# A two-block transformer kernel on one core: the first stage laid out by features

## Chip, cores and metric

The kernel runs on one core of one Trainium2 chip. Its time is the device time of one execution in microseconds (us); the median of several executions is given. Engines are named as in the profile: PE is the matrix engine, DVE the vector engine, ACT the scalar engine, POOL is GpSimd, and SP issues the transfers.

## What is computed

Two transformer blocks on a sequence of 512 tokens with 1024 features, all in float32. Only the head of the first block is touched by the change:

```python
cs = silu(c)                                      # c: (1, 1024)
shift, scale, gate = split(cs @ w_mod + b_mod, 3) # w_mod: (1024, 3072)
h = x * (1 + scale) + shift                       # x: (512, 1024)
q, k, v, r, a_lr = split(h @ gla_w_in, ...)       # gla_w_in: (1024, 3088)
# gated linear attention with 4 heads (keys of 128, values of 256 features),
# layer norm, a gated convolutional MLP with its own modulation;
# second block: a retention layer and an attention layer on latent keys
```

## The kernel before

**Products.** A float32 operand is kept as two parts, `hi` and `lo` (`split`: a cast on ACT, then a subtraction on DVE). A product of two such operands is three matmuls into the same PSUM accumulator, `hi*hi`, `hi*lo` and `lo*hi` (`mm3`, lines 137 to 139). A weight tile is loaded as `raw`, cast by ACT into `wsp` (L97) and completed by DVE (L98, the `lo` part). The product of 128 features with a tile of 512 columns is thus three matmuls of 512 columns.

**First stage** (`gla_start`). It goes over the features in four quarters of 256. Per quarter, `scales` loads eight 128-row slices of the 256 columns of `scale` and of `shift` (`ms`), multiplies each by its value of silu(c) and adds it to `macc` (L487, eight instructions on DVE). `macc` then holds 128 partial sums per column, one on each partition. Four transposes on PE (L359) and a reduction on DVE (L360) turn them into columns (`mc`) that lie along partitions. The quarter of x (`xq`) arrives with tokens on partitions, and eight transposes on PE (L509) bring its features there; ACT applies scale and shift from PSUM twice (L513, once into `hT` hi and once into `xv`), and DVE forms the `lo` part (L514). Then come the projections of this quarter into six PSUM banks: v of the first two heads (four banks, one for each block of 128 tokens), q and k of head 0 (two banks). The other two banks serve the transposes.

**After it**: `gla_a` (24 matmuls with the 16 gate columns `was`), `gla_r` (96 matmuls with the output gates), the decays (`gla_decay`: four float32 matmuls L576, exponential and logarithm on ACT, then L587), and the heads. `gla_qk` projects q and k of a further head, 48 matmuls for each head. `gla_inner` of a head holds a chain of narrow products and small DVE work (`qd`, `ki`, `kt`, `af`, `at`, `sf`, `st`), `gla_outer` the outputs `po`. The place of the program where the heads begin reads

```python
p0 = prep(0)
raw += self.gla_qk(xT, (1,))
p1 = prep(1)
place(3)
i0 = self.gla_inner(ph, p0, vh(0), tril)
raw += self.gla_qk(xT, (2,))
i1 = self.gla_inner(ph, p1, vh(1), tril)
raw += self.gla_qk(xT, (3,))
```

`place` puts in six further pieces of the modulation (`mod_chunk`: four loads `rawm`, eight DVE instructions on `macc` each). They share the four `raw` buffers with the weights. A scheduler makes each engine's order out of the written program; each engine then executes its own list in order. All loads are issued by SP in one list; a load waits there for its buffer, and no more than eight loads are under way at a time.

Of the kernel before, what the change touches and what calls it, by code (L numbers as in the profile page):

```python
# [10 lines left out]
F32 = mybir.dt.float32  # L11
F32R = mybir.dt.float32r
# [6 lines left out]
P = 128  # L19
T = 512  # L20
# [48 lines left out]

class Pair:  # L70
    """hi and lo parts of an operand whose contraction runs over k-tiles of 128 partitions"""
# [8 lines left out]
class Kern:  # L80
# [5 lines left out]
    # ------------------------------------------------------------------ helpers  # L86
# [36 lines left out]
    def wsubs(self, w, c0, c1, k0=0, k1=None, gain=None, pool=None, main=0):  # L123
        """weights w[k0*128:k1*128, c0:c1] in pieces; the first `main` ones always from the main pool"""
# [16 lines left out]
    def psum(self, nacc):  # L141
        """PSUM banks: nacc for the accumulators of projections, the others for all else"""
# [41 lines left out]
    def proj_f(self, xT, tiles, evict, halves=1, nk=8, width=P):  # L184
        """features on partitions: tiles yields the pieces of one feature tile; evict(n, psum[width, 512 tokens])"""
# [23 lines left out]
    def rsqrt(self, v):  # L209
        """1/sqrt(v) for v[128, n] > 0, in float32"""  # L210
# [15 lines left out]
    def transpose_split(self, dst, src, b, split_copy=True):  # L226
        """src [128 tokens, 1024] -> the columns of block b of the k-tiles in dst (Pair tiles [hi|lo][128, 4, 512])"""
# [20 lines left out]
    # ------------------------------------------------------------------ program  # L248
# [5 lines left out]
    def run(self):  # L254
        tc, nc = self.tc, self.nc
        with ExitStack() as ctx:
# [4 lines left out]
            with self.psum(6) as self.ps:  # L261
                next(gla)
# [16 lines left out]
    def setup(self, ph):  # L279
        nc, a = self.nc, self.a  # L280
        cr = ph.tile([8, P], F32, name="cr")
        nc.sync.dma_start(cr, a["c"].rearrange("o (k p) -> (o k) p", p=P))
# [4 lines left out]
        nc.vector.memset(self.ones, 1.0)  # L287
        self.cs = self.cons.tile([P, 8], F32, name="cs")
        cst = ph.tile([8, P], F32, name="cst")
        nc.scalar.activation(cst, cr, AF.Silu)  # L290
        ps = self.aux()
        nc.tensor.transpose(ps[:, :8], cst, self.ident[:8, :8])
        nc.vector.tensor_copy(self.cs, ps[:, :8])
        self.res = [None] * NB
        self.col = {}

    def vectors(self, ph):
        """vectors over features as columns of 128 partitions"""
# [30 lines left out]
    def mod_chunk(self, i, c0, pool=None, tag="raw", bufs=0):  # L329
        """[128, 512] whose column sums are (silu(c) @ mod_w[0, i] + mod_b[0, i])[c0:c0 + 512]"""  # L330
# [18 lines left out]
    def mod_bcast(self, acc):  # L349
        """column sums on all partitions: PSUM [128, 512]"""  # L350
# [4 lines left out]
    def mod_cols(self, acc, out):  # L355
        """column sums as columns: out[128, 4]"""
# [11 lines left out]
    # ------------------------------------------------------------------ GLA  # L368
    def gla(self):
        nc, a, tc = self.nc, self.a, self.tc  # L370
        w = a["gla_w_in"][0]
        with ExitStack() as ctx:
# [27 lines left out]
            with tc.tile_pool(name="gla_core", bufs=1, reuse_waits="tile") as ph:  # L400
# [22 lines left out]
                raw += self.gla_qk(xT, (1,))  # L423
# [25 lines left out]
            # scale and shift of the sublayer that follows  # L449
# [15 lines left out]
    def gla_start(self, ph, out):  # L465
        """x * (1 + scale) + shift, features on partitions, a quarter of the features at a time, and the first
        projections on each quarter: v of the first pair of heads, q and k of the first head"""
        nc, a = self.nc, self.a
        w = a["gla_w_in"][0]
        tl, xT = self.new_hT()  # L470
        accs = [self.acc() for _ in range(6)]
        Q = 256

        def scales(q):
            """1 + scale and shift of a quarter as columns [128, 4], and the quarter of x"""
            c0 = q * Q
            acc = self.mod.tile([P, 512], F32, tag="macc", name="macc", bufs=self.MACC)
            nc.gpsimd.memset(acc, 0.0)
            for j, c in enumerate((1024 + c0, c0)):
                nc.sync.dma_start(acc[0:1, j * Q:(j + 1) * Q], a["mod_b"][0, 0:1, c:c + Q])  # L480
            for k0 in (0, 4):
                raw = ph.tile([P, 4, 2, Q], F32, tag="ms", name="ms", bufs=5)
                for j, c in enumerate((1024 + c0, c0)):
                    nc.sync.dma_start(raw[:, :, j, :], a["mod_w"][0, 0, k0 * P:(k0 + 4) * P, c:c + Q]
                                      .rearrange("(k p) n -> p k n", p=P))
                for k in range(4):
                    nc.vector.scalar_tensor_tensor(acc, raw[:, k].rearrange("p j n -> p (j n)"),  # L487
                                                   self.cs[:, k0 + k:k0 + k + 1], acc, op0=OP.mult, op1=OP.add)
            xq = self.main.tile([P, NB, Q], F32, tag=f"res{q}", name=f"xq{q}")
            nc.sync.dma_start(xq, a["x"][0][:, c0:c0 + Q].rearrange("(b p) n -> p b n", p=P))  # L490
            mc = self.small(4, "mc")
            self.mod_cols(acc, mc)
            nc.vector.tensor_scalar_add(mc[:, 0:2], mc[:, 0:2], 1.0)
            return mc, xq

        def weights(q):
            c0 = q * Q
            return (self.wload([(0, w[c0:c0 + Q, 1024:1536])], 2, 512),
                    self.wload([(0, w[c0:c0 + Q, 0:P]), (P, w[c0:c0 + Q, 512:512 + P])], 2, 2 * P))

        ahead = [scales(0)]
        ws = [weights(0)]
        for q in range(4):
            mc, xq = ahead.pop(0)
            for i in range(2):
                k = 2 * q + i
                px = self.aux()
                for b in range(NB):
                    nc.tensor.transpose(px[:, b * P:(b + 1) * P], xq[:, b, i * P:(i + 1) * P], self.ident)  # L509
                hi, lo = tl[k // 4][:, 0, k % 4, :], tl[k // 4][:, 1, k % 4, :]  # L510
                v = ph.tile([P, T], F32, tag="t2", name="xv", bufs=2)
                for d in (hi, v):
                    nc.scalar.activation(d, px, AF.Identity, scale=mc[:, i:i + 1], bias=mc[:, 2 + i:3 + i])  # L513
                nc.vector.tensor_sub(lo, v, self.f(hi))  # L514
            if q < 3:
                ahead.append(scales(q + 1))
                ws.append(weights(q + 1))
            wv, wqk = ws.pop(0)
            for b in range(NB):
                for i in range(2):  # L520
                    l = [t[:, b * P:(b + 1) * P] for t in xT.k[2 * q + i]]
# [755 lines left out]
```

## Time and profile before

| what | value |
|---|---|
| median of 3 runs | 1274.15 us (1274.1 to 1274.72) |
| span of the profiled execution, first to last instruction | 1272.2 us |
| PE busy | 1239.5 us, 97% of the span |
| DVE busy | 825.5 us, 65% |
| ACT busy | 526.6 us, 41% |
| data moved | 147.83 MB, mean 116 GB/s |

The profiled execution has no time of its own beside its span, so the sums are made against the span; the median of the runs is 1.95 us above it, which is what lies before the first and after the last instruction, and a saving inside the span is carried over to the median as it is. PE counts as busy from the start of a matmul to its modelled end, and matmuls overlap: one of 512 columns shows 0.39 us, and the next one starts 0.23 us after it.

### The profile page before, as it was taken

Reading aid. Unit: us, or ns where it says so; the run is one execution under the profiler, and the core shown is the slowest. Engines: PE = TensorE matmul, PEld = TensorE weight load, DVE = VectorE, ACT = ScalarE, POOL = GpSimd, SP = SyncE. Lnnn points to the kernel's source line nnn. Section 1 sums busy time; section 2 is a strip of 40 time slices with the busy share of each in tenths; the row PEclk is TensorE's granted clock in tenths of the full one; section 3 lists DMA queues with packets and bytes.
Section 4 is the critical chain, followed back from the end, with each engine's and each line's share of the span. In section 5 each row is a group of like instructions: output and inputs, shape, how many; then the busy total and the mean of one; then the engine's idle time right before and its main releaser. Section 6 shows DMA issues by size and latency. Waiting matters only on the chain.

```text
span 1272.2 us, 16374 instructions
## 1 busy us (share of the span) xinstructions
PE 1239.5 (97%) x6123; PEld 1038.8 (82%) x6123; DVE 825.5 (65%) x1838; ACT 526.6 (41%) x930; POOL 8.8 (1%) x22
## 2 busy tenths in 40 slices
PE   4999999999999999999999999999999999999997
PEld 3778877898888888888788888888888889888886
DVE  6968696788543344454884747647454689686755
ACT  3437344353332123342443343423433447476631
POOL 1000000000000000000000000000000000000000
PEclk9999999999999999999999999999999999999999
DMA  9785262517433333325143232233332333212221
GB/s 313 227 256 173 83 220 67 161 42 226 131 99 99 99 99 100 98 90 162 66 149 91 82 97 80 80 94 92 117 116 99 108 97 96 85 47 73 74 93 67
DMA packets 145695, 147.83 MB, mean 116 GB/s; under 512 B 9223, under 2 KB 106030, under 8 KB 145615
## 3 DMA queue, kind: packets, MB, share of 16 engines
q1 hardware_dynamic: 145614, 146.78, 37.3%
q8 instruction: 48, 0.79, 0.3%
q14 instruction: 33, 0.26, 0.1%
HBM read 140.47 MB, written 6.29 MB: 115 GB/s over the span
## 4 chain that ended last, share of the span: by engine, by line
PE 83%; DVE 5%; ACT 2%; issue 1%; DMA 0%; DVEq 0%; ACTq 0%
PE acc L139 24%; PE acc L137 24%; PE acc L138 24%; PE po L137 1%; PE po L139 1%; PE po L138 1%; PE aux L139 1%; PE aux L137 1%; PE aux L138 1%; DVE wsp L98 1%; PE aux L872 1%; PE aux L1241 1%; PE aux L700 0%; ACT hv L709 0%; DVE rs_t L219 0%
## 5 line engine op out<-in xcount | busy, mean ns | idle before, releaser
L98 DVE TENSOR_TENSOR wsp<-raw,wsp 128x1024 fp32r<-128x1024 f32 (+1 forms) x164 | 196.0, 1196 | 197.1 <-ACT wsp L97 196.8
L97 ACT CAST wsp<-raw 128x1024 fp32r<-128x1024 f32 (+1 forms) x164 | 168.6, 1030 | 314.7 <-PE acc L139 253.6
L137 PE MATMUL acc<-hT,wsp 128*128 128x512 f32 (+1 forms) x640 | 244.6, 382 | 0.0
L139 PE MATMUL acc<-hT,wsp 128*128 128x512 f32 (+1 forms) x640 | 244.0, 381 | 0.0
L138 PE MATMUL acc<-hT,wsp 128*128 128x512 f32 (+1 forms) x640 | 243.5, 380 | 0.0
L137 PE MATMUL acc<-wsp,hT 128*128 128x512 f32 (+2 forms) x448 | 172.8, 386 | 2.6 <-ACT hT L513 2.6
L138 PE MATMUL acc<-wsp,hT 128*128 128x512 f32 (+2 forms) x448 | 171.6, 383 | 0.0
L139 PE MATMUL acc<-wsp,hT 128*128 128x512 f32 (+2 forms) x448 | 169.2, 381 | 0.0
L137 PEld LDWEIGHTS acc<-hT,wsp 128*128 128x128 f32 x640 | 121.0, 189 | 22.7 <-issue 0.8
L138 PEld LDWEIGHTS acc<-hT,wsp 128*128 128x128 f32 x640 | 121.0, 189 | 22.1 <-issue 0.2
L139 PEld LDWEIGHTS acc<-hT,wsp 128*128 128x128 f32 x640 | 120.8, 189 | 22.2
L137 PEld LDWEIGHTS acc<-wsp,hT 128*128 128x128 f32 x448 | 84.7, 189 | 19.0 <-ACT hT L513 3.6
L139 PEld LDWEIGHTS acc<-wsp,hT 128*128 128x128 f32 x448 | 84.1, 188 | 15.2
L138 PEld LDWEIGHTS acc<-wsp,hT 128*128 128x128 f32 x448 | 84.8, 189 | 14.1
L137 PE MATMUL acc<-wsp,uT 128*128 128x512 f32 (+1 forms) x192 | 74.6, 389 | 0.0
L139 PE MATMUL acc<-wsp,uT 128*128 128x512 f32 (+1 forms) x192 | 74.6, 388 | 0.0
L138 PE MATMUL acc<-wsp,uT 128*128 128x512 f32 (+1 forms) x192 | 74.4, 387 | 0.0
L137 PE MATMUL acc<-wsp,p 128*128 128x512 f32 x144 | 56.1, 389 | 0.0
L138 PE MATMUL acc<-wsp,p 128*128 128x512 f32 x144 | 56.1, 389 | 0.0
L139 PE MATMUL acc<-wsp,p 128*128 128x512 f32 x144 | 56.1, 389 | 0.0
L774 DVE SCALAR_TENSOR_TENSOR cv<-acc,cols,cv 128x511 f32<-128x511 f32 x22 | 16.5, 749 | 57.1 <-ACT cv L773 57.1
L342 DVE SCALAR_TENSOR_TENSOR macc<-rawm,cs,macc 128x512 f32<-128x512 f32 x64 | 47.9, 749 | 8.3 <-DMA rawm<-in_mod_w 7.3
(364 smaller groups left out, 2081.4 us busy)
## 6 DMA issues: line engine op xcount, KB each, us to landing
raw<-in_w_in_a SPq DMA_DIRECT2D x48, 512.0 KB
raw<-in_ffn_w_up SPq DMA_DIRECT2D x44, 512.0 KB
rawm<-in_mod_w SPq DMA_DIRECT2D x32, 512.0 KB
raw<-in_gla_w_in SPq DMA_DIRECT2D x22, 512.0 KB
raw<-in_ffn_w_down SPq DMA_DIRECT2D x22, 512.0 KB
ms<-in_mod_w SPq DMA_DIRECT2D x16, 512.0 KB
raw<-in_w_out_a SPq DMA_DIRECT2D x16, 512.0 KB
raw<-in_gla_w_o SPq DMA_DIRECT2D x8, 512.0 KB
```

Source lines behind the costliest of these rows:

```text
L97: nc.scalar.copy(hi, src)
L98: nc.vector.tensor_sub(lo, src, self.f(hi))
L137: mm(out, l[0], r[0], start=first, stop=False)
L138: mm(out, l[0], r[1], start=False, stop=False)
L139: mm(out, l[1], r[0], start=False, stop=last)
L342: nc.vector.scalar_tensor_tensor(acc, raw[:, k, :], self.cs[:, k0 + k:k0 + k + 1], acc, op0=OP.mult, op1=OP.add)
L774: nc.vector.scalar_tensor_tensor(t[:, 1:], p[:, :T - 1], cw[NT + j], t[:, 1:], op0=OP.mult, op1=OP.add)
L872: nc.tensor.transpose(pu[:, b * P:(b + 1) * P], u[:, b, i * P:(i + 1) * P], self.ident)
L1241: nc.tensor.transpose(pt[:, (b - j) * P:(b - j + 1) * P], pr[b][:, j * P:(j + 1) * P], self.ident)
```

## The change

Five arrays are laid out anew outside the kernel, as further inputs: x transposed (`l_x`, features as rows), the scale and shift columns of the first modulation matrix transposed and side by side (`l_mod`, 1024 rows of 2048), their bias as columns (`l_modb`), c as columns (`l_c`), and the weight columns of v of heads 0 and 1, q of heads 0 and 1 and k of heads 0 and 1 side by side (`l_w`, 1024 rows of 1024). The first stage goes over the features in eight steps of 128. In each, two instructions on DVE multiply 1024 values of a row by silu(c), which lies on all partitions (`csr`, one load that reads the same 4 KB for every partition), and return the sum of the row as well (`accum_out`). No transposes are left in this stage. Per step the projections are four blocks of v and four tiles of q and k of heads 0 and 1, in eight PSUM banks; the later `gla_qk` of head 1 is gone. silu(c) as columns, which the later pieces of the modulation need, is loaded after the stage. Comments and docstrings that the change drops as well are left out here.

```diff
+def layouts(ins):
+    w, m, b = ins["gla_w_in"][0], ins["mod_w"][0, 0], ins["mod_b"][0, 0]
+    both = np.concatenate([m[:, 1024:2048].T, m[:, 0:1024].T], 1)
+    bias = np.stack([b[1024:2048].reshape(8, P), b[0:1024].reshape(8, P)], -1)
+    return {"l_x": np.ascontiguousarray(ins["x"][0].T),
+            "l_mod": np.ascontiguousarray(both),
+            "l_modb": np.ascontiguousarray(bias.transpose(1, 0, 2).reshape(P, 16)),
+            "l_c": np.ascontiguousarray(ins["c"].reshape(8, P).T),
+            "l_w": np.ascontiguousarray(np.concatenate([w[:, 1024:1536], w[:, 0:256], w[:, 512:768]], 1))}
...
-            with self.psum(6) as self.ps:
+            with self.psum(8) as self.ps:
                 next(gla)
...
+        self.csr = ph.tile([P, D], F32, name="csr")
+        nc.sync.dma_start(self.csr, bass.AP(tensor=cr.tensor, offset=cr.offset, ap=[[0, P], [1, D]]))
+        nc.scalar.activation(self.csr, self.csr, AF.Silu)
...
                 p0 = prep(0)
-                raw += self.gla_qk(xT, (1,))
                 p1 = prep(1)
...
+        def loads(k):
+            r = slice(k * P, k * P + P)
+            m = ph.tile([P, 2, D], F32, tag="ms", name="ms", bufs=4)
+            for j in range(2):
+                nc.sync.dma_start(m[:, j], a["l_mod"][r, j * D:(j + 1) * D])
+            nc.sync.dma_start(xs[k // 2][:, k % 2], a["l_x"][r])
+            raw = self.main.tile([P, self.WN], F32, tag="raw", name="raw", bufs=self.RAW)
+            nc.sync.dma_start(raw, a["l_w"][r])
+            return m, raw
+        def operand(k, m):
+            mc = self.small(2, "mc")
+            for j in range(2):
+                nc.vector.scalar_tensor_tensor(m[:, j], m[:, j], 1.0, self.csr, op0=OP.mult, op1=OP.mult,
+                                               accum_out=mc[:, j:j + 1])
+            nc.vector.tensor_scalar(mc[:, 0:1], mc[:, 0:1], mb[:, k, 0:1], 1.0, op0=OP.add, op1=OP.add)
+            nc.vector.tensor_add(mc[:, 1:2], mc[:, 1:2], mb[:, k, 1:2])
+            x = xs[k // 2][:, k % 2]
+            hi, lo = tl[k // 4][:, 0, k % 4, :], tl[k // 4][:, 1, k % 4, :]
+            v = ph.tile([P, T], F32, tag="t2", name="xv", bufs=2)
+            for d in (hi, v):
+                nc.scalar.activation(d, x, AF.Identity, scale=mc[:, 0:1], bias=mc[:, 1:2])
+            nc.vector.tensor_sub(lo, v, self.f(hi))
...
+        for k in range(8):
+            m, raw = loads(k)
+            operand(k, m)
+            sp = weights(raw)
+            wv = [sp[:, i, 0:512] for i in range(2)]
             for b in range(NB):
+                self.mm3(accs[b], [t[:, b * P:(b + 1) * P] for t in xT.k[k]], wv, k == 0, k == 7)
+            for j in range(4):
+                self.mm3(accs[4 + j], [sp[:, i, 512 + j * P:640 + j * P] for i in range(2)], xT.k[k], k == 0, k == 7)
```

**First place: DVE inside the first stage.** Before, DVE's list for one quarter (256 features) reads (`macc` the partial sums, `mc` the columns of scale and shift, `wsp` the weights, `hT` the operand):

```order
L487 SCALAR_TENSOR_TENSOR macc<-ms,cs,macc 128x512 x7
L98 TENSOR_TENSOR wsp<-raw,wsp 128x1024
L360 TENSOR_REDUCE mc<-aux 128x4
L98 TENSOR_TENSOR wsp<-raw,wsp 128x512
L493 TENSOR_SCALAR mc<-mc 128x2
L514 TENSOR_TENSOR hT<-xv,hT 128x512
L487 SCALAR_TENSOR_TENSOR macc<-ms,cs,macc 128x512
L514 TENSOR_TENSOR hT<-xv,hT 128x512
```

Of the change, DVE's list from the second sum of the third step of 128 features to the operand of the fourth:

```order
L504 SCALAR_TENSOR_TENSOR ms,mc<-ms,csr 128x1024
L506 TENSOR_SCALAR mc<-mc,mb 128x1
L507 TENSOR_TENSOR mc<-mc,mb 128x1
L513 TENSOR_TENSOR hT<-xv,hT 128x512
L504 SCALAR_TENSOR_TENSOR ms,mc<-ms,csr 128x1024
L111 TENSOR_TENSOR wsp<-raw,wsp 128x1024
L504 SCALAR_TENSOR_TENSOR ms,mc<-ms,csr 128x1024
L506 TENSOR_SCALAR mc<-mc,mb 128x1
L507 TENSOR_TENSOR mc<-mc,mb 128x1
L111 TENSOR_TENSOR wsp<-raw,wsp 128x1024
L504 SCALAR_TENSOR_TENSOR ms,mc<-ms,csr 128x1024
L513 TENSOR_TENSOR hT<-xv,hT 128x512
```

In the change the operand of a step (L513) stands in some steps right behind its two column operations, so that DVE has to wait there for ACT, and in others (the second L513 here) behind a weight subtraction and the next step's first sum.

**Second place: PE behind the first head's `gla_inner`.** Before, the last narrow products of head 0 (`aux<-v,kt`) are followed by 46 projection matmuls of head 2, of which the first rows are:

```order
L138 MATMUL aux<-v,kt 128x256
L139 MATMUL aux<-v,kt 128x256
L139 MATMUL acc<-hT,wsp 128x512
L137 MATMUL acc<-hT,wsp 128x512
L138 MATMUL acc<-hT,wsp 128x512
```

Of the change, the same place:

```order
L151 MATMUL aux<-v,kt 128x256
L152 MATMUL aux<-v,kt 128x256
L151 MATMUL acc<-hT,wsp 128x512
L150 MATMUL aux<-qd,ki 128x128
L151 MATMUL aux<-qd,ki 128x128
L152 MATMUL aux<-qd,ki 128x128
```

One projection matmul is left between head 0's narrow products and those of head 1; head 1's own are cut by four more, and 39 of head 3 come behind them.

**Third place: SP behind the first stage.** Before, SP's list of loads behind the first stage (`wa` the gate columns, `rawm` a piece of the modulation, `raw` the weights of `gla_r`) reads:

```order
L555 DMA wa<-in_gla_w_in 128x8x16
L334 DMA macc<-in_mod_b 1x512
L339 DMA rawm<-in_mod_w 128x2x512 x4
L110 DMA raw<-in_gla_w_in 128x2x512 x2
L334 DMA macc<-in_mod_b 1x512
```

Of the change:

```order
L310 DMA cs<-in_l_c 128x8
L561 DMA wa<-in_gla_w_in 128x8x16
L350 DMA macc<-in_mod_b 1x512
L355 DMA rawm<-in_mod_w 128x2x512 x4
L123 DMA raw<-in_gla_w_in 128x2x512
L350 DMA macc<-in_mod_b 1x512
```

The order is the same but for the small load of `cs` ahead of it, and the second weight tile of `gla_r`, which moved behind the next bias row.

## Rows read from the trace of the kernel before

**Rows 1.** The page's first line.

```profile
span 1272.2 us, 16374 instructions
```

**Rows 2.** First stage in stretches: busy us and count by engine, PEclk granted clock, DMA share.

```profile
0.00:18.53 18.53, 3.28 (x13) 2.46 (x13) 10.08 (x16) 3.99 (x6) 4.32 (x15) 1.00 0.91 287
18.53:30.50 11.97, 11.20 (x50) 9.10 (x49) 9.05 (x14) 4.36 (x7) 0.53 (x1) 1.00 1.10 349
30.50:41.90 11.40, 10.12 (x48) 7.91 (x48) 9.62 (x14) 4.35 (x7) 0.52 (x1) 1.00 1.09 350
41.90:53.31 11.41, 10.13 (x49) 7.88 (x49) 10.51 (x17) 4.54 (x8) 0.53 (x1) 1.00 0.48 133
53.31:61.60 8.29, 8.29 (x36) 6.78 (x37) 7.96 (x12) 6.12 (x10) 0.00 (x0) 1.00 0.69 233
```

**Rows 3.** PE's waits over the whole run: us in total, times, longest us.

```profile
PE aux L359 <- DVE macc L487: 11.2, 1, 11.2
...
PE acc L137 <- ACT hT L513: 2.6, 3, 0.9
...
PE aux L509 <- DVE mc L360: 2.0, 3, 1.2
...
PE aux L137 <- DVE af L630: 1.3, 2, 0.8
```

**Rows 4.** PE in order of time: start us, us, instruction [idle before it].

```profile
18.53 0.80 PE L137 MATMUL acc<-wsp,hT 128*128 128x512 f32 x1
...
21.26 0.53 PE L137 MATMUL acc<-wsp,hT 128*128 128x512 f32 x1
...
61.62 0.40 PE L137 MATMUL acc<-hT,was 128*16 128x512 f32 x1
...
89.07 0.69 PE L576 MATMUL aux<-wa,arow 17*128 17x512 f32 x1
```

**Rows 5.** SP in order of time, at the very start.

```profile
0.74 0.40 SPq L282 DMA_DIRECT2D cr<-in_c  x1
...
1.21 0.40 SPq L484 DMA_DIRECT2D ms<-in_mod_w  x1
```

**Rows 6.** Two stretches of 1 us, same columns as Rows 2.

```profile
2.00:3.00 1.00, 0.18 (x1) 0.18 (x1) 0.00 (x0) 0.34 (x2) 1.00 (x3) 1.00 0.63 101
...
1219.00:1220.00 1.00, 1.00 (x7) 0.81 (x6) 0.24 (x1) 0.00 (x0) 0.00 (x0) 1.00 1.01 410
```

**Rows 7.** DVE by line and shape: count | busy us, mean ns | idle before.

```profile
L487 DVE SCALAR_TENSOR_TENSOR macc<-ms,cs,macc 128x512 f32<-128x512 f32 x32 | 24.0, 751 | 5.8 <-DMA ms<-in_mod_w 5.0
...
L98 DVE TENSOR_TENSOR wsp<-raw,wsp 128x1024 fp32r<-128x1024 f32 x156 | 190.6, 1222 | 197.1 <-ACT wsp L97 196.8
...
L678 DVE SCALAR_TENSOR_TENSOR res<-res,z 128x512 f32<-128x512 f32 x16 | 10.7, 689 | 0.2
...
L678 DVE DVE_READ_ACCUMULATOR res<-res,z 128x1 f32 x16 | 1.3, 84 | 0.0
...
L810 DVE SCALAR_TENSOR_TENSOR res<-res,z 128x512 f32<-128x512 f32 x8 | 5.1, 684 | 0.0
...
L997 DVE SCALAR_TENSOR_TENSOR res<-y,rs_y,res 128x1024 f32<-128x1024 f32 x7 | 9.0, 1285 | 0.2
```

**Rows 8.** ACT by line and shape, same columns.

```profile
L97 ACT CAST wsp<-raw 128x1024 fp32r<-128x1024 f32 x156 | 163.9, 1051 | 306.1 <-PE acc L139 245.5 <-DMA raw<-in_gla_w_in 34.0 <-issue 14.4
...
L513 ACT ACTIVATE hT<-aux,mc 128x512 fp32r<-128x512 f32 x8 | 6.2, 777 | 19.1 <-PE aux L509 12.5 <-DVE mc L493 6.7
```

**Rows 9.** DVE in order of time around head 0's `gla_inner`.

```profile
113.00 0.55 DVE L98 TENSOR_TENSOR kt<-aux,kt 128x384 fp32r<-128x384 f32 x1
...
120.90 0.42 DVE L638 TENSOR_TENSOR sf<-aux,sf 128x256 f32<-128x256 f32 x1
```

**Rows 10.** PE in order of time inside head 0's `gla_inner`.

```profile
112.32 0.28 PE L139 MATMUL aux<-qd,ki 128*128 128x128 f32 x1
...
112.99 0.28 PE L139 MATMUL aux<-qd,ki 128*128 128x128 f32 x1
```

More of the change, by code (lines that the diff above doesn't have):

```diff
@@ L286, in setup, with setup_late @@
         self.ones = self.cons.tile([P, P], F32, name="ones")
[L287 to L293, printed above, removed]
+        nc.gpsimd.memset(self.ones, 1.0)
         self.res = [None] * NB
         self.col = {}
+    def setup_late(self, ph):
+        nc, a = self.nc, self.a
+        self.cs = self.cons.tile([P, 8], F32, name="cs")
+        nc.sync.dma_start(self.cs, a["l_c"])
+        nc.scalar.activation(self.cs, self.cs, AF.Silu)
     def vectors(self, ph):
@@ L468, in gla_start @@
         nc, a = self.nc, self.a
-        w = a["gla_w_in"][0]
         tl, xT = self.new_hT()
[L471 to L518, printed above, removed]
-            for b in range(NB):
-                for i in range(2):
-                    l = [t[:, b * P:(b + 1) * P] for t in xT.k[2 * q + i]]
-                    self.mm3(accs[b], l, wv[i], q + i == 0, q + i == 4)
-            for j in range(2):
-                for i in range(2):
-                    l = [t[:, j * P:(j + 1) * P] for t in wqk[i]]
-                    self.mm3(accs[4 + j], l, xT.k[2 * q + i], q + i == 0, q + i == 4)
@@ new lines, in gla_start @@
+        accs = [self.acc() for _ in range(8)]
+        mb = ph.tile([P, 8, 2], F32, name="mb")
+        nc.sync.dma_start(mb, a["l_modb"].rearrange("p (k j) -> p k j", j=2))
+        xs = [self.main.tile([P, 2, T], F32, tag=f"res{q}", name=f"xq{q}") for q in range(4)]
+        def loads(k):
[7 more added lines that the diff above has]
+            return m, raw
@@ new lines, in weights @@
+        def weights(raw):
+            sp = self.main.tile([P, 2, self.WN], F32R, tag="wsp", name="wsp", bufs=self.WSP)
+            self.split(sp[:, 0], sp[:, 1], raw)
+            return sp
+        for k in range(8):
[3 more added lines that the diff above has]
+            wv = [sp[:, i, 0:512] for i in range(2)]
+            for b in range(NB):
+                self.mm3(accs[b], [t[:, b * P:(b + 1) * P] for t in xT.k[k]], wv, k == 0, k == 7)
+            for j in range(4):
+                self.mm3(accs[4 + j], [sp[:, i, 512 + j * P:640 + j * P] for i in range(2)], xT.k[k], k == 0, k == 7)
@@ L529, in gla_start @@
             self.split(v[:, 0, b, :], v[:, 1, b, :], accs[b])
-        raw = self.main.tile([P, 2, T], F32, tag="res0", name="qk0")
-        for j in range(2):
-            nc.scalar.copy(raw[:, j], accs[4 + j])
-        return xT, v, [raw]
+        raws = []
+        for h in range(2):
+            raw = self.main.tile([P, 2, T], F32, tag=f"res{h}", name=f"qk{h}")
+            for j in range(2):
+                nc.scalar.copy(raw[:, j], accs[4 + 2 * j + h])
+            raws.append(raw)
+        self.setup_late(ph)
+        return xT, v, raws
     def gla_v(self, out, xT, pr):
@@ L571, in gla_decay @@
         nc.sync.dma_start(cum, a["k_cum"])
-        la = ph.tile([P, NB, 512], F32, tag="ms", name="la", bufs=5)
-        e = ph.tile([P, NB, 512], F32, tag="ms", name="lz", bufs=5)
+        la = ph.tile([P, NB, 512], F32, tag="ms", name="la", bufs=4)
+        e = ph.tile([P, NB, 512], F32, tag="ms", name="lz", bufs=4)
         for b in range(NB):
@@ L1273 @@
     ins.update(constants())
+    ins.update(layouts(ins))
     build(nc, ins)
```

3 lines of the change are left out of this document (1 added, 2 removed).

## The prediction, made before the result was known

> **What bounds the kernel now.** I read the page first, then the first stage in stretches, PE's waits, and PE in order of time. The reader is to see that the span [rows 1] is PE's nearly everywhere but not at its head: PE is busy for 3.28 of the first 18.53 us, and in the two middle quarters for about 10.1 of 11.4 us [rows 2]. It waits once for 11.2 us until the first column sums are there, and later, at the three further quarters, 2.6 us for ACT's operand and 2.0 us for the reduced columns [rows 3]. Its 48 transposes in the stage count as busy, but are no product. From the 16-column product at 61.62 to the float32 product at 89.07 lie 120 matmuls without a gap: 27.45 / 120 = 0.229 us each [rows 4]. So the price of a 512-column matmul on PE's path is 0.229 us, and whatever else PE does or waits for in the stage is loss.
>
> Before, the stage's 144 matmuls are 33.0 us of the 61.6 us; 28.6 us are waits, transposes and a slow start. The six starts from 18.53 to 21.26 lie 0.455 us apart, though the granted clock in that stretch reads 1.00 [rows 2, 4]: the first matmuls go at about half the pace.
>
> **The change, part by part.**
>
> *Work that only moves.* q and k of head 1 are 48 matmuls, 11.0 us, that stood behind the decays and now stand in the stage. So the kernel before must be compared at 61.6 + 11.0 = 72.6 us. The stage of the change holds 192 matmuls: 43.9 us.
>
> *When PE can start.* A load issued at 1.21 shows as 101 GB/s in the stretch 2 to 3 us; at the later 350 GB/s that is 0.3 us of flow, so bytes flow 1.5 us after the issue [rows 2, 5, 6]. `csr`, issued at 0.74, flows from 2.2. Ahead of the first product lie `csr` 0.52 MB, two rows of the modulation 1.05, x 0.26, weights 0.52: 2.36 MB. Before, the stage's loads in runs of 512 B to 2 KB ran at 350 GB/s; loads in 4 KB runs late in the kernel show 410 [rows 2, 6]. Most bytes now come in 4 KB runs; with 370 the landings are 3.7 (`csr`), 5.1 and 6.5 (the two halves), 7.2 (x), 8.6 (weights). Silu of `csr` takes about as long as a cast of that size, 1.05 us [rows 8], and is done before the first half lands.
>
> *One column sum.* No row of before shows the 1024-wide form with an accumulated sum. The 512-wide form with two float32 sources on chip takes 0.689 us with the sum and 0.684 without; reading the sum out takes 0.084. The step from 512 to 1024 columns is 1.285 - 0.751 = 0.534 us [rows 7]. So 0.689 + 0.534 + 0.084 = 1.3 us. The bounds are 1.2, if the read-out overlaps, and 2.4, if the sum goes at half rate at this width (one more time 1.07).
>
> The Trainium skill has a rule for just this form: "Vector Engine (DVE) Microarchitecture Reference", section "Points that are easy to get wrong", says that this instruction with two sources in SBUF that are not bf16 runs at half throughput, since both read ports are taken and none is left for the accumulator. By it a sum would cost 2.4 us and the change would lose; the 512-wide row with the sum, 5 ns slower than the one without, speaks against it.
>
> *The chain through DVE.* A step has two sums (2.6), two column operations (0.3 with hand-over, an estimate from the 84 ns of a one-column instruction), the weights' `lo` (1.2) and the operand's `lo` (0.65, a 512-wide instruction) [rows 7]: 4.75 us. Where the operand's `lo` stands right behind the columns (the order at the first place), DVE also waits for ACT's two passes, 2 x 0.777 [rows 8], 1.6 us: 6.35. The list has four such steps (second, third, fifth, seventh); the others cost 4.75. First step: sums from 5.2, columns at 8.2, ACT to 9.9, operand done at 10.6. The last also has its own weights' `lo` ahead of its operand's, and some wait: 1.6 more. The eighth is done at 10.6 + 4 x 6.35 + 3 x 4.75 + 1.6 = 51.9. PE needs it for the second matmul of the last step: 51.9 + 23 x 0.229 = 57.2.
>
> *The chain through PE.* Its first matmul needs ACT's operand (9.1) and, behind ACT's second pass, the cast weights: 10.9 against 18.53. From there 43.9 us of matmuls, 1.8 for eight at half pace, 0.6 where a step's `lo` is late: 57.2. The two chains end together, so each will sometimes wait for the other; I add 0.8 and take **58.0**. Loads bind less: 2.2 + 15.2 MB at 370 GB/s is 43.3. At 283 GB/s they would end at 55.9, and with cast and matmuls the stage at 62.5.
>
> Gain at this point: 72.6 - 58.0 = **14.6 us**.
>
> *Behind the stage: weights of `gla_r`.* All eight banks hold sums when the stage ends. DVE's list has two sums of the next piece, four `lo` of v, five more, and only then the first weights' `lo`: 5 x 0.75 + 1.2 behind the last v at about 59.4 gives 64.4; PE, after 24 matmuls of the gate, is there at 63.5. Loss **0.9**, from 0 to 2. SP's list (third place) puts the second tile later, but its 5.5 us of matmuls ahead cover it.
>
> *Behind the decays.* Before, 33 matmuls of head 1 stand over exponential and logarithm; now 35 of head 2. No change taken, 1 us either way.
>
> *Where the moved work was a cover.* After head 0's narrow products came 46 matmuls, 10.5 us of cover for DVE; now head 1's narrow products follow (second place). A head's second weight needs the four spare banks back. Before, DVE went from `kt` at 113.00 to the end of the third `sf` at 121.3 without a pause: 8.3 us [rows 9]. Of the change, that list has no weight (-1.1) but `af`, `kt` and `at` of head 1 (+1.7): 8.9 us. PE's own work to the same place is 21 narrow matmuls at 0.112 [rows 10], three transposes, four wide ones and six more narrow: about 5 us from 1.2 us after the start. So PE idles some 3.6 us, where before it lost about 1.0 of its 1.3 us of waits for `af` [rows 3]. Loss **2.6**, from 0 to 8: if DVE's whole backlog showed (two heads' chains, some 22 us of DVE work against 24 us of PE work with 39 wide matmuls as cover), 5 us more.
>
> **Sum.** 14.6 - 0.9 - 2.6 = 11.1 us. Span 1272.2 - 11.1 = 1261.1; median 1274.15 - 11.1 = **1263.0**.
>
> **Rivals.**
>
> *Handed back among the heads.* The stage is as short as said, but DVE, busy without pause where the heads begin, can't follow, and PE idles 8 us there. For it: rows 9 show no slack in DVE's list. Against: 39 matmuls of head 3 stand ahead of the outputs. 14.6 - 0.9 - 8 = 5.7: 1268.5.
>
> *The stage bound by loads.* 14.68 MB in place of 13.6, and one load that reads a single row 128 times. At 283 GB/s the stage ends at 62.5: gain 10.1 - 3.5 = 6.6, 1267.5. Against: 350 GB/s in the shorter runs of before [rows 2].
>
> *Sums at half rate: slower.* At 2.4 us each sum costs 1.1 more, sixteen of them 17 us on DVE's chain: stage end 57.2 + 17 + 0.8 = 75, loss 2.4 + 3.5 = 5.9, 1280. It decides from a sum of 2.0 us on: then 16 x 0.7 = 11 us are gone, the whole gain. Against: the 689 ns row [rows 7]. It is the case that the rule of the Trainium skill named above would bring about.
>
> *Nothing changes.* The columns come sooner, but PE loses as much as it wins in stalls that I don't see: 1274. I see no place for 11 us.
>
> **How the numbers follow.** Chances: the forecast (1259 to 1266) 0.62; handed back 0.16; loads 0.11; half rate 0.06; nothing 0.05. The range reaches down to 1258.5, no loss behind the stage at all (14.6 + 0.8), and up to 1270, which takes in most of the two middle rivals: about 0.8. A measurement can tell about 0.2%, 2.5 us. Faster by more than that: 0.62 + 0.16 + 0.11 and a little of the last, 0.89; same 0.04; slower 0.07.
>
> **What would show it.** Right: PE's first wide matmul at about 11; column sums of 1.2 to 1.3 us; the 16-column product at 57 to 60; a PE gap before the weights of `gla_r` below 2 us; some 4 us of waits for `af`, `sf` or `kt` between the two heads, before 115. Wrong: a sum above 2 us; DVE waiting for loads in each step; or PE idle for more than 6 us between the heads.

## The result, and the profile after

The median of four runs is 1262.34 us (1261.62 to 1263.42), against 1274.12 us (1273.82 to 1274.72): 11.8 us less, a ratio of 0.991 with a 95% interval of 0.9898 to 0.9921. The forecast was 1263.0. The profiled span fell by 12.4 us, from 1272.2 [rows 1]; the execution that was profiled is the shortest of the four, 1261.62. The page of the changed kernel begins with its span, and its fourth part is the chain that ended last, by engine:

```profile
span 1259.8 us, 16234 instructions
...
PE 90%; DVE 5%; ACT 2%; DMA 1%; issue 1%; SPq 0%; DVEq 0%; ACTq 0%
```

PE's waits over the whole run (us in total, times, longest), to be laid beside [rows 3]:

```profile
PE acc L150 <- ACT wsp L110: 13.3, 1, 13.3
PE aux L150 <- ACT kt L110: 0.9, 1, 0.9
PE aux L246 <- DVE res L1003: 0.9, 2, 0.6
PE aux L150 <- DVE sf L644: 0.7, 1, 0.7
PE aux L152 <- DVE kt L111: 0.6, 1, 0.6
...
PE aux L150 <- DVE af L636: 0.5, 1, 0.5
```

There is one wait of 13.3 us at the very start, and none in the rest of the stage. The same in stretches (columns as in [rows 2]): the start, the first 5.7 us of PE's work, and the rest of the stage.

```profile
0.00:13.26 13.26, 0.00 (x0) 0.00 (x0) 4.10 (x9) 4.79 (x5) 3.95 (x15) 1.00 0.82 281
13.26:19.00 5.74, 5.74 (x14) 4.26 (x15) 4.15 (x9) 2.17 (x3) 0.00 (x0) 1.00 1.04 415
19.00:59.55 40.55, 40.55 (x181) 33.47 (x179) 32.22 (x59) 19.39 (x28) 0.00 (x0) 1.00 0.81 292
```

PE is busy for 40.55 of 40.55 us from 19.00 on, where before a middle quarter held 10.1 of 11.4. The second stretch is slower: 14 matmuls in 5.74 us, 0.41 us each. Where the gain is made and where some of it goes is read from the same instructions in both kernels. After (PE in order of time):

```profile
59.55 0.40 PE L150 MATMUL acc<-hT,was 128*16 128x512 f32 x1
...
86.97 3.75 PE L582 MATMUL aux<-wa,arow 17*128 17x512 f32 x8
...
100.61 3.92 PE L593 MATMUL aux<-cum,la 128*128 128x128 f32 x32
...
154.49 1.91 PE L434 MATMUL aux<-ident,u 128*128 128x128 f32 x16
```

Of before, the first two stand in [rows 4] (61.62 and 89.07); the other two read:

```profile
103.39 0.82 PE L587 MATMUL aux<-cum,la 128*128 128x128 f32 x5 [1.29 <-DVE la L582]
...
167.43 1.91 PE L418 MATMUL aux<-ident,u 128*128 128x128 f32 x16
```

| place | before, with the matmuls by which the change is ahead in its work there (48, 48, 50 and none, 0.229 us each) | after | gain so far |
|---|---|---|---|
| 16-column product, stage end | 61.62 + 11.0 = 72.6 | 59.55 | 13.05 |
| first product of the decays | 89.07 + 11.0 = 100.1 | 86.97 | 13.1 |
| `cum` products, behind the decays | 103.39 + 11.45 = 114.8 | 100.61 | 14.2 |
| first transposes of the gates, behind the first heads | 167.43 | 154.49 | 12.9 |

At the third place the kernel before has done 33 of head 1's 48 matmuls, and the change all of them and 35 of head 2's, which makes the 50. So the stage makes 13.05 us, the decays add 1.1 (the wait of 1.29 us for `la` is gone), and the heads take 1.3 back. PE's last matmul is 13.0 us earlier too (1264.69 and 1251.71); the span's 12.4 holds a tail behind it that is 0.6 us longer in this execution (7.8 against 7.2 us).

### The profile page after: what moved, and what is told of

It is laid out like the page before. It is cut to its first block, busy times and chain, and to the rows that moved or that the text cites. A ratio compares the mean times of both kernels' runs of the same rounds, so it can differ in the third digit from the quotient of the medians.

```text
span 1259.8 us, 16234 instructions
## 1 busy us (share of the span) xinstructions
PE 1232.7 (98%) x6074; PEld 1032.9 (82%) x6074; DVE 817.6 (65%) x1842; ACT 528.5 (42%) x929; POOL 6.9 (1%) x19
## 4 chain that ended last, share of the span: by engine, by line
PE 90%; DVE 5%; ACT 2%; DMA 1%; issue 1%; SPq 0%; DVEq 0%; ACTq 0%
PE acc L150 27%; PE acc L152 27%; PE acc L151 26%; PE po L150 1%; PE po L152 1%; PE po L151 1%; PE aux L150 1%; PE aux L152 1%; PE aux L151 1%; DVE wsp L111 1%; PE aux L878 1%; PE aux L1247 1%; DMA ms<-in_l_mod 0%; PE aux L706 0%; ACT hv L715 0%
## 5 line engine op out<-in xcount | busy, mean ns | idle before, releaser
L150 PE MATMUL acc<-wsp,hT 128*128 128x512 f32 (+2 forms) x448 | 169.8, 385 | 13.3 <-ACT wsp L110 13.3
L150 PEld LDWEIGHTS acc<-wsp,hT 128*128 128x128 f32 x448 | 84.6, 189 | 28.7 <-ACT wsp L110 13.3
L358 DVE SCALAR_TENSOR_TENSOR macc<-rawm,cs,macc 128x512 f32<-128x512 f32 x64 | 47.8, 749 | 11.1 <-DMA rawm<-in_mod_w 9.8
```

The source lines that it names most:

```text
L150: mm(out, l[0], r[0], start=first, stop=False)
L358: nc.vector.scalar_tensor_tensor(acc, raw[:, k, :], self.cs[:, k0 + k:k0 + k + 1], acc, op0=OP.mult, op1=OP.add)
```

## Experiments

The theory at the start: the whole gain is made in the first stage, by PE's waits and transposes that are gone, and PE alone now sets the stage's end. Rivals: the gain is that of x's layout alone (no transposes); or head 1's work, moved into the stage, carries part of it. Each time stands beside that of the kernel before on the same chip (1273.67 for the first four, 1273.56 for the next four, 1273.41 for `rows128` and `all_four`).

### `six_banks`: the change without the moved work

```diff
-        accs = [self.acc() for _ in range(8)]
+        accs = [self.acc() for _ in range(6)]
...
                 p0 = prep(0)
+                raw += self.gla_qk(xT, (1,))
```

> The change without the moved work: q and k of head 1 go back to their old place between the heads, the stage has six accumulators and weight tiles of 768 columns. Theory (the stage gains by what PE loses no more; the 48 matmuls of head 1 only move, and cover DVE's chain there): PE alone would end the stage at 13.3 + 33.0 + 2.4 = 48.7 us, but DVE's list has eight steps of about 4.15 us and waits for ACT in four of them behind the first, which puts the eighth operand at about 48.4 and the stage's end, 17 matmuls later, at about 52.3. That is 3.8 us later than the change's 59.55 less 11.0, and 0.8 us come back between the heads: 1264 to 1267 us. Rival (PE sets the end with or without head 1's work, the move gains nothing): stage end below 49.5 and 1261 to 1262.5 us.

Measured: 1265.6 us, ratio 0.9935 (0.992 to 0.995). The stage ends at 52.64 (52.3 expected), 4.1 us later than the change's 59.55 - 11.0; 0.7 of that is a later start, since the first load landed later in this execution (first wide matmul at 13.96, in the change at 13.26). DVE's waits in this stage:

```profile
DVE hT L514 <- ACT xv L513: 7.9, 5, 1.6
```

PE waits three more times within the stage, 2.0 us in all, for weights whose cast is late. So with 18 matmuls a step PE is faster than the chain through DVE and ACT; head 1's six more fill PE's time. The rival that head 1's work carries part of the gain holds: some 3.4 of the 13 us at the stage's end need it. Nothing was returned among the heads (gate transposes at 158.65, also 4.2 us later), where 0.8 had been expected.

### `mod_only` and `x_only`: the two layouts apart

`mod_only` is `six_banks` with x loaded as before and transposed on PE; `x_only` is the kernel before with x loaded transposed:

```diff
...
-            nc.sync.dma_start(xq, a["x"][0][:, c0:c0 + Q].rearrange("(b p) n -> p b n", p=P))
+            nc.sync.dma_start(xq, a["l_x"][c0:c0 + Q].rearrange("(i p) n -> p i n", p=P))
...
-                px = self.aux()
-                for b in range(NB):
-                    nc.tensor.transpose(px[:, b * P:(b + 1) * P], xq[:, b, i * P:(i + 1) * P], self.ident)
+                px = xq[:, i]
```

> Only the modulation is laid out by features: x comes with tokens on partitions and is transposed on PE, 32 transposes in the stage; six accumulators, head 1's q and k in their old place. Theory: PE's first wide matmul stays near 13.3 us, the transposes cost their 3.6 us on PE, and the stage ends near 52 us; 1264.5 to 1267 us, so this part alone makes 7 to 10 of the 12 us. Rival (the gain lies in the layout of x, the transposes and what waits on them): 1270 us or more.

> Only x is laid out by features: the kernel before with x loaded transposed and its 32 transposes on PE gone; the modulation keeps its partial sums on partitions. Theory: the first wide matmul comes at most 1 us earlier than 18.53, because the partial sums of the first quarter set it, and a quarter stays bound by DVE at about 10 us in place of 11.4: gain 1.5 to 5.5 us, 1269 to 1272.5 us. Rival (the layout of x is the gain): 1262 to 1265 us.

Measured: `mod_only` 1269.35 us, 0.9963 (0.995 to 0.9976), below the gain that the theory gave; its stage ends at 55.14, 2.5 us behind `six_banks`, 1.1 of it at the start (first wide matmul at 15.04, not near 13.3). `x_only` 1276.31 us, **slower**, 1.0021 (1.0011 to 1.0032): no theory had that. PE's waits in its stage, and two stretches behind the third of them:

```profile
PE acc L137 <- ACT hT L511: 8.9, 4, 2.8
...
42.00:44.00 2.00, 1.86 (x5) 1.53 (x6) 1.18 (x2) 2.00 (x4) 0.00 (x0) 0.64 1.13 252
44.00:46.00 2.00, 2.00 (x6) 1.52 (x6) 1.97 (x4) 1.86 (x4) 0.00 (x0) 0.51 0.96 355
46.00:48.00 2.00, 2.00 (x11) 1.61 (x10) 1.89 (x4) 0.00 (x0) 0.00 (x0) 1.00 0.15 49
```

Before, PE transposed x while the column sums went through DVE and ACT. Without the transposes it stands still in that time, 2.0 us a quarter (the 8.9 less 2.8 at the first, over three), because the chain from the partial sums to ACT's operand sets the pace of a quarter. And behind two of these pauses PE's granted clock (third column from the right) falls to its lower level, 1.2 GHz, for about 3.4 us each, 1.7 us lost each time. The stage ends at 64.65, 3.0 us later than before, in an execution of 1278.82 us, the longest of the eight. Without the 3.4 us lost to the clock it would end 0.4 us earlier than before (an estimate). So the transposes cost next to nothing as long as the modulation came by partial sums. With the modulation's new layout they do: the step from `mod_only` to `six_banks` is 3.75 us. The gain of 11.8 is 4.3 for the modulation without x, 3.75 more for x, and 3.3 more for the moved work (from 1265.6 to 1262.3; across two chips, where the kernel before reads 0.5 us apart). `mod_only` also has the weights side by side and eight steps in place of four quarters; what these two are worth by themselves was not measured.

### `sums32`: every column sum twice

```diff
+            for j in range(2):
+                scr = ph.tile([P, D], F32, tag="scr", name="scr")
+                nc.vector.scalar_tensor_tensor(scr, m[:, j], 1.0, self.csr, op0=OP.mult, op1=OP.mult,
+                                               accum_out=mc[:, j:j + 1])
```

> The change with each of its sixteen column sums taken twice (the first time into a scratch tile), 16 x 1.2 = 19 us more work on DVE in the stage. If DVE's list kept its waits for ACT, the eighth operand would come 19 us later, at 70, the stage would end at 76 and the time would be about 1278.6 us, slower than before: the size that the rival of the half rate gave. If the longer list fills these waits (its order has other sums between the columns and the operand), a step takes 6.7 us without a wait, the eighth operand comes at 61.5 and the stage ends at about 67: 1269 to 1271 us. If DVE's chain had nothing to do with the stage's end: 1262 us.

Measured: 1269.88 us, 0.9964 (0.995 to 0.9978), the middle case. The stage ends at 67.57, 8.0 us later, for 18 us more work on DVE; 1.3 of the 8.0 is a later landing (first sum at 9.21, in the change at 7.91). DVE in two stretches (third pair is DVE):

```profile
20.00:30.00 10.00, 10.00 (x44) 7.99 (x43) 10.00 (x20) 4.94 (x6) 0.00 (x0) 1.00 1.03 406
...
40.00:50.00 10.00, 8.49 (x36) 6.34 (x35) 10.00 (x20) 6.17 (x9) 0.00 (x0) 1.00 0.53 146
```

DVE is busy without a gap: the 8.4 us that it waited for ACT in the change are filled, because the scheduler laid other sums between the columns and the operand. With twice the sums a gain of 3.8 us is left, in the order that the scheduler made for them. Sums that cost twice as much in the change's own order, where the waits for ACT stay, were not measured.

### `csr_rows`, `mb_late`, `csr_pe`, `hold_back`: why PE starts at 13.3

In the change, the flow of the first microseconds (last column GB/s); from 3 to 5 us it falls to 160 GB/s, which the expectations call the trough. The first half is the first of the two loads of a step's modulation (`ms`).

```profile
2.00:3.00 1.00, 0.00 (x0) 0.00 (x0) 0.00 (x0) 0.02 (x1) 1.00 (x4) 1.00 1.02 381
3.00:4.00 1.00, 0.00 (x0) 0.00 (x0) 0.00 (x0) 0.00 (x0) 1.00 (x4) 1.00 0.57 160
4.00:5.00 1.00, 0.00 (x0) 0.00 (x0) 0.00 (x0) 0.70 (x1) 0.50 (x2) 1.00 0.74 160
5.00:6.00 1.00, 0.00 (x0) 0.00 (x0) 0.00 (x0) 0.35 (x1) 0.00 (x0) 1.00 0.91 250
6.00:7.00 1.00, 0.00 (x0) 0.00 (x0) 0.00 (x0) 0.00 (x0) 0.00 (x0) 1.00 1.01 354
```

Four kernels ask what makes the trough and the late first half. `csr_rows` changes the source of one load, to a new input that holds the row 128 times; `mb_late` moves one load down; `csr_pe` spreads c by PE; `hold_back` writes one column of each later target from the first half, so that these loads wait for it (six such copies, of which one is shown).

```diff
# csr_rows
-        nc.sync.dma_start(self.csr, bass.AP(tensor=cr.tensor, offset=cr.offset, ap=[[0, P], [1, D]]))
+        nc.sync.dma_start(self.csr, a["l_cr"])
# csr_pe
+        nc.sync.dma_start(c1, a["c"])
...
+            nc.tensor.matmul(pc, self.ones[0:1, :], c1[:, j * 512:(j + 1) * 512], start=True, stop=True)
+            nc.scalar.activation(self.csr[:, j * 512:(j + 1) * 512], pc, AF.Silu)
# hold_back
...
+                    nc.vector.tensor_copy(m[:, j, 0:1], first[0])
```

> The change with csr loaded from an array that holds the row 128 times (each partition reads its own 4 KB), nothing else. In the change's profile the bytes flow at 344 to 418 GB/s from 2 to 3 us, at 130 to 190 from 3 to 5, and at over 340 from 6 on; the first half of the modulation lands at 7.9. If the 128 reads of the same 4 KB make that trough, it is gone: the first half lands at 5.5 to 6.5, PE starts at 11.3 to 12.3 in place of 13.26, and the time falls by 1 to 2 us to about 1261. If they don't, start and time stay as they are (13.0 to 13.5 us, 1262.3 us).

> The change with the bias columns mb (8 KB, 128 pieces of 64 bytes) issued behind the four loads of the first step in place of ahead of them. If the small pieces make the trough, the first half of the modulation lands at 5.5 to 6.5 and PE starts near 12; if not, the first half comes about 0.5 us earlier by the earlier issue alone, PE starts at 12.7 to 13.3, and the time stays within 0.6 us of 1262.3.

> The change with c loaded as one row of 4 KB, spread over the partitions by two float32 matmuls with ones, and silu taken from PSUM: 0.52 MB fewer bytes ahead of the first step. By both theories of the trough the first half of the modulation lands earlier, by 1.3 us (0.52 MB at 400 GB/s) if only the bytes count and by 2 to 3 us if the load of csr makes the trough; csr itself is then ready at about 7 (row at 3, two cold matmuls, two passes of ACT). PE's first wide matmul at 10.5 to 12.3, time 1259.5 to 1261.3 us.

> The change with the loads behind the first half of the modulation held back until that half has landed (each target gets one column written from it first; only two constants of 64 KB go ahead), to see how long csr and one half take alone. In the change the half lands at 7.91 after 1.7 MB have moved in all, so 0.6 MB of later loads had moved by then; in other executions with the same order it lands between 7.2 and 9.2. If it is late because the later loads share the flow with it, it now lands when csr, the half and the small loads are through: 1.2 MB, which the change had moved at 6.6, so at 6.2 to 6.8 or earlier. If the first half megabytes are slow by themselves, whoever else moves, it lands at 7.2 or later. The time is not the point: PE starts later, at 15 to 16, and the time rises by 2 to 4 us.

| kernel | first sum starts | PE's first wide matmul | stage end | time (ratio, interval) |
|---|---|---|---|---|
| the change | 7.91 | 13.26 | 59.55 | 1262.34 (0.991, 0.9898 to 0.9921) |
| `csr_rows` | 7.80 | 13.16 | 58.91 | 1261.56 (0.9904, 0.9888 to 0.9921) |
| `mb_late` | 7.39 | 12.36 | 57.90 | 1262.73 (0.9913, 0.9898 to 0.9928) |
| `csr_pe` | 6.83 | 11.94 | 58.90 | 1260.92 (0.9901, 0.9886 to 0.9916) |
| `hold_back` | 6.57 | 14.65 | 60.60 | 1264.1 (one execution; before 1276.03) |

The 128 reads of one row are not the cause: `csr_rows` flows at 221, 365, 254 and 242 GB/s over 2 to 6 us, moves 1.08 MB there against 0.95, and its first half comes 0.1 us earlier. The small pieces are not the cause either: with `mb` behind, the half comes 0.5 us earlier, as the earlier issue gives (PE starts at 12.36, earlier than the 12.7 to 13.3 expected, and the time is the same). In `csr_pe` the first sum waits until 6.83 for `csr`; the half itself is complete at 5.74, by the trace's landings, 2.1 us earlier than the change's 7.80. That is more than 0.52 MB take at 400 GB/s, 1.3 us, and what they take at the 250 GB/s of these microseconds; whether the load of `csr` also slows the flow stays open. `hold_back` shows the larger part; DVE's first wait for the half is now

```profile
DVE ms L500 <- DMA ms<-in_l_mod: 4.8, 1, 4.8
```

against 6.5 us: the half is there at 6.18, 1.7 us earlier, once the loads issued behind it don't flow beside it. The rest, 1.1 us to the forecast's 5.1, is a slow flow of the first megabyte (230 to 271 GB/s from 3 to 6 us in `hold_back`); what makes it stays open. PE starts at 14.65 in `hold_back`, a little ahead of the 15 to 16 expected, and the time, 11.9 us under the kernel before on its chip as in the change, did not rise by the 2 to 4 us expected. These are single executions, and the landing varies between them: the first sum starts at 7.2 to 9.2 in six kernels whose list of loads begins alike (`warm` 7.22, the change 7.91, `rows128` 8.78, `six_banks` 8.81, `mod_only` 8.89, `sums32` 9.21). The 1.7 us of `hold_back` is thus 1.0 to 3.0, by the execution that it is set against. The half lands in 16 pieces, and the spread is in the last of them: nine are there by 6.5 in the change and in `rows128`, the sixteenth at 7.8 and 8.7; in `csr_pe` all sixteen come between 5.2 and 5.7.

### `warm`: PE kept busy ahead of the stage

```diff
-        nc.gpsimd.memset(self.ones, 1.0)
+        nc.vector.memset(self.ones, 1.0)
...
+        wz = ph.tile([P, T], F32, tag="t2", name="wz", bufs=2)
+        nc.vector.memset(wz, 1.0)
+        for _ in range(11):
+            nc.tensor.matmul(accs[7], self.ones, wz, start=True, stop=True)
```

> The change with eleven float32 matmuls of ones ahead of the stage, into a bank that the stage overwrites later. In the change the first matmuls start 0.43 us apart, not 0.23, and the stage's 192 matmuls take 46.3 us in place of 43.9. If PE is slow there because it stood idle until then, the first wide matmuls come 0.23 us apart, the 16-column product starts 2 us earlier than 59.55 and the time is about 1260.3 us. If the slow start has another cause (operands that come late), the spacing and the time stay; if the eleven last longer than 13.3 us, they delay the start by what is over.

Measured: 1263.1 us, 0.9919 (0.9904 to 0.9933). The eleven (22 matmuls for PE) and the first wide matmuls of `warm`:

```profile
1.60 12.38 PE L489 MATMUL acc<-wz,ones 128*128 128x512 f32 x22 [1.60 <-DVE wz L487]
13.42 1.48 PE L150 MATMUL acc<-wsp,hT 128*128 128x512 f32 x4
14.74 0.39 PE L150 MATMUL acc<-hT,wsp 128*128 128x512 f32 x1
14.96 0.39 PE L151 MATMUL acc<-hT,wsp 128*128 128x512 f32 x1
```

They stand 0.22 to 0.23 us apart from 14.74 on, as everywhere later, and the stage ends at 58.19, 1.36 us earlier. So the slow start is PE's, from standing idle, and not one of late operands. Two things take from the 2 us expected: the eleven last until 13.98 and hold the first wide matmul up by 0.9 us, whose weights are cast at 12.53; and ahead of the 16-column product PE waits 0.68 us for ACT's copy of `qk`. The median shows nothing of the gain: at the gate transposes 0.1 us is left (154.40). Between 59 and 100 us PE waits 0.7 us more, for cast weights, in `warm` and never in the change, and from 88 to 96 us the granted clock is low for longer: 6.8 us at half pace in `warm`, 3.4 in the change. The next kernel takes that up.

### `rows128`: the decays over 128 rows

```diff
-        arow = ph.tile([17, T], F32, name="arow")
+        arow = ph.tile([P, T], F32, name="arow")
...
-        wa2 = ph.tile([17, 512], F32, name="wa2")
+        wa2 = ph.tile([P, 512], F32, name="wa2")
+        nc.gpsimd.memset(wa2, 0.0)
```

> The change with the four float32 products of the decays over 128 rows (111 of them zeros) in place of 17. In the change these take 3.7 us from 86.97 on, and then PE's granted clock reads 0.50 from 90.5 to 93.7: 3.3 us at half pace, 1.6 us lost; in the profiles of two experiments it stays low for twice as long, 3.4 us lost. If it falls because so few of PE's rows work there, it now stays at 1.00 through that place, PE is 1.6 us earlier behind it, and the time is 1260 to 1261 us with less spread between runs. If the float32 form itself or the gap-free change of form makes it fall, clock and time stay as in the change, 1262.3 us.

Measured: 1261.88 us, 0.9907 (0.9892 to 0.9922). Two stretches of the change, then of `rows128` (first pair PE, third column from the right the granted clock):

```profile
88.00:92.00 4.00, 3.98 (x10) 1.47 (x8) 3.25 (x5) 3.61 (x6) 0.00 (x0) 0.81 0.80 220
92.00:96.00 4.00, 4.00 (x14) 3.22 (x15) 2.17 (x3) 3.97 (x4) 0.00 (x0) 0.76 0.96 256
```

```profile
88.00:92.00 4.00, 3.41 (x10) 1.44 (x9) 3.67 (x6) 3.74 (x6) 0.00 (x0) 1.00 0.99 268
92.00:96.00 4.00, 4.00 (x19) 3.30 (x18) 1.85 (x3) 3.97 (x4) 0.00 (x0) 1.00 0.97 259
```

The clock does as expected: behind the float32 products with 17 rows it falls to 1.2 GHz, with 128 rows it stays at 2.4. The few rows are not the whole of it, though: in `x_only` it stays at 2.4 behind the same products with 17 rows (92.11 to 95.80), and falls at 107.4, behind a wait of 2.35 us:

```profile
92.11:95.80 3.69, 3.69 (x10) 1.47 (x9) 2.83 (x4) 1.60 (x3) 0.00 (x0) 1.00 1.14 311
95.80:103.40 7.60, 7.60 (x34) 6.23 (x34) 5.44 (x7) 7.55 (x8) 0.00 (x0) 1.00 0.89 241
106.10:112.00 5.90, 5.90 (x35) 5.78 (x36) 4.74 (x12) 4.44 (x8) 0.00 (x0) 0.71 0.41 133
```

In `rows128` the 1.7 us don't come off the time. PE now waits there, 0.6 us for a weight's `lo` and 1.0 for `la`, which it did not before; from the first product of the decays to the `cum` products it takes 13.55 us against 13.64. So the chain through ACT and DVE sets this place, and the slow clock had only filled PE's wait.

### `all_four`: c by PE, four matmuls of ones, 128 rows

The edits of `csr_pe`, `warm` (four in place of eleven) and `rows128` together.

> The change with c spread by PE, four float32 matmuls of ones behind that, and the 128 rows in the decays. If the parts add up: first wide matmul at 11.9 us at full pace, stage end 59.55 - 1.3 - 2.0 = 56.2 us, the first transposes of the gates at 154.5 - 1.3 - 2.0 - 1.6 = 149.6, time 1257 to 1258.5 us. If what is won ahead of the heads is handed back there (DVE has no pause where the heads begin, and the loads come no earlier), the stage still ends near 56.2 but the transposes stand at 152 to 153 and the time at 1260 to 1261 us.

Measured: 1258.49 us, 0.9882 (0.9865 to 0.9898). PE in order of time:

```profile
11.98 1.20 PE L150 MATMUL acc<-wsp,hT 128*128 128x512 f32 x4 [0.49 <-ACT wsp L110]
13.01 0.39 PE L150 MATMUL acc<-hT,wsp 128*128 128x512 f32 x1
...
55.66 0.40 PE L150 MATMUL acc<-hT,was 128*16 128x512 f32 x1
...
151.59 1.91 PE L438 MATMUL aux<-ident,u 128*128 128x128 f32 x16
```

The stage ends 3.9 us earlier than the change's and the gate transposes come 2.9 earlier: the stage as expected, the transposes between the two expectations, the time at the upper end of the first. About 1 us of the stage's gain is handed back at the decays and the heads, where PE's waits from 84 to 152 us are 4.4 us against 1.5. Still, this version beats both kernels by the medians, the change by 3.9 us (3.1 when each is set against the kernel before on its own chip).

## Why the prediction was right, step by step

**The sum.** Forecast 14.6 for the stage, less 0.9, less 2.6: 11.1. Measured 13.05, plus 1.1, less 1.3: 12.9 at the gate transposes, 11.8 in the medians. That the total came out close is in part luck: errors of opposite sign cancelled, a stage that ends 1.55 us later than said, and losses behind it of 0.1 us in all in place of 3.5.

**When PE can start: mis-sized, 10.9 against 13.26.** `csr` landed at 4.3 (3.7 said), the first half at 7.9 (5.1). The failed step is "Ahead of the first product lie ..." with landings one after the other at 370 GB/s: several loads flow side by side, so an early one is finished only when 1.7 MB have moved in place of 1.05 (`hold_back`: 1.7 us, of single executions), and the first megabyte flows slower than later ones (1.1 us). Later the flow is faster than the 370 taken, 405 from 20 to 30 us.

**The slow start.** 1.8 us said, 2.4 measured: the stage's 192 matmuls take 46.3 us (from 13.26 to 59.55) in place of 43.9. `warm` shows that it is PE's pace after idling.

**One column sum: 1.3 said, 1.14 from start to start, just under the lower bound of 1.2.** By shape, on DVE (count, busy us, mean ns):

```profile
L504 DVE SCALAR_TENSOR_TENSOR ms<-ms,csr 128x1024 f32<-128x1024 f32 x16 | 19.5, 1220 | 6.6 <-DMA ms<-in_l_mod 6.5
...
L504 DVE DVE_READ_ACCUMULATOR ms<-ms,csr 128x1 f32 x16 | 1.3, 83 | 0.0
```

The read-out begins before the sum's modelled end. The rule of the Trainium skill ("Vector Engine (DVE) Microarchitecture Reference", section "Points that are easy to get wrong") that this form runs at half throughput does not hold for this instruction: 1220 ns with the sum is what 1222 ns is for a 1024-wide subtraction without one [rows 7].

**The chain through DVE.** The waits of 1.6 us for ACT are there, in the four steps named, the first step too, and 0.45 in the last; 8.4 us in all. Two steps take 10.1 us (operands at 24.28, 34.42 and 44.55), 11.1 said. The eighth operand is done at 51.1 (51.9 said), although the first came 2.4 us late.

**"Both chains end together": no.** PE never waited inside the stage, the 0.8 us set aside were not needed, and the eighth operand was some 3 us early. 58.0 was said, 59.55 measured: 2.4 us from the late start and 0.6 from the slow one, less the 0.8 and the 0.6 for late `lo` parts that were not needed. That the 48 moved matmuls are what makes PE the bound was not in the prediction; it took them as work that only moves, and `six_banks` shows some 3.4 us at the stage's end that need them.

**Weights of `gla_r`: 0.9 said, nothing measured.** From the 16-column product to the first product of the decays PE takes 27.42 us, 27.45 before. **Decays:** plus 1.1, where 1 us either way was allowed.

**The cover between the heads: 2.6 said, 1.3 measured.** Of the waits in the page's list only those for `kt` are at the place named, 1.6 us; the kernel before waits 1.0 us between its `cum` products and its gates. Of the change, then of before:

```profile
111.65 0.39 PE L152 MATMUL aux<-v,kt 128*128 128x256 f32 x1 [0.63 <-DVE kt L111]
...
116.47 0.39 PE L150 MATMUL aux<-v,kt 128*128 128x256 f32 x1 [0.94 <-ACT kt L110]
```

```profile
127.68 0.39 PE L137 MATMUL aux<-v,kt 128*128 128x256 f32 x1 [0.18 <-ACT kt L97]
...
129.25 0.39 PE L137 MATMUL aux<-v,kt 128*128 128x256 f32 x1 [0.82 <-DVE af L630]
```

The waits for `af` (0.5) and `sf` (0.7) come at 160.79 and 164.99, behind the gate transposes, and stand in the kernel before as well (0.49 at 173.63, 0.66 at 177.84). Waits thus explain 0.6 of the 1.3; where the rest goes stays open. The step was mis-sized, and partly in its own sum: 8.9 us of DVE less PE's 5 us from 1.2 us on leave PE idle for 2.7 us, not 3.6, and the loss would be 1.7.

**The rivals.** Loads: no, PE waits for none after its start. Handed back: not in the change, but `rows128` and `all_four` show the mechanism, 1 us of 3.9. Half rate: the sums are at full rate. The price that it was given (slower from 2.0 us per sum on) stays untested: `sums32` doubles the sums and stays 0.36% faster than before, but its longer list has another order, in which the waits for ACT are filled, while the prediction's price holds DVE's order as it was.

## What to carry to other kernels

Transposes on the matrix engine that lay beside a longer chain were all but free here; taking them away alone made this kernel 2.6 us slower, and paid only once that chain was short. A short stage is worth filling with products from a later place, as long as the engine there is the one that idles (3 to 4 us here). Price a first load by all the bytes that move before it lands, not by those ahead of it in the list, and look behind a place won for the chain that sets the next one before counting a gain (`rows128`: 3.4 us of half clock gone, 0.1 us gained at that place).

## What the runs showed of the hardware that was not expected

- Four float32 products with 17 of 128 rows, 3.7 us of "busy" PE, are followed in the change by 3.3 us at a granted clock of 0.50 (1.2 GHz), with matmuls 0.43 to 0.65 us apart. In the executions profiled here the clock is low from about their end on (from 1.9 us before it to 1.8 us behind it) for 3.4 us (before, the change, `six_banks`, `mod_only`, `mb_late`, `csr_pe`) or for twice as long (6.8 us in `sums32`, `csr_rows`, `warm`, `hold_back`), and not at all with 128 rows, 111 of them zeros (`rows128`, `all_four`). One execution goes against it: in `x_only` the 17-row products are not followed by a low clock, which comes 11.6 us later.
- At the start of the stage the matmuls are 0.43 us apart while the granted clock reads 1.00. They are as far apart where it reads 0.50 (before, 93.70 to 95.84), and the trace's first record of the clock is at 18.80, where the spacing changes to 0.23: until then the 1.00 is not a measurement, and the spacing is the better witness. The Trainium skill ("TensorE: Matmul & The Clock Gate", section "Part 1: The HAM clock gate") says that the slow pace is the default and activity lifts it; `warm` agrees, 0.22 us from 14.74 on.
- With `csr` as the first load the flow from 3 to 6 us is 111 to 287 GB/s (365 in one microsecond of `csr_rows`); with `c` as a row of 4 KB it is at 422 from 5 to 6 us (`csr_pe`, `all_four`). From 20 to 30 us it is 398 to 407 in all of them. Why stays open.
